# The context's exponentials in an attention loop: their low parts move from GpSimd to VectorE, behind the maxima

## The chip, the cores and the metric

The kernel runs on one core of a Trainium2 chip. A core has TensorE (matrix products, "PE" in the profile, with its weight loads "PEld"), VectorE ("DVE"), ScalarE ("ACT"), GpSimd ("POOL") and SyncE ("SP", which issues most DMAs here). Each has its own queue of instructions and works through it in order; between engines there are only semaphores. The metric is the device time of one execution in microseconds (us), the median over the runs shown.

## What is computed

One layer of an image generator: a modulated RMS norm, one input projection, two groups of heads, and one output projection added to the input. The part that matters here is the attention over 1024 tokens (a grid of 16 x 64) and 256 context tokens, with 8 heads of 64.

```python
s_lat = jnp.einsum('biqhd,birkhd->bhiqrk', q_rot, k_rows,
                   preferred_element_type=jnp.float32) * scale + bias
s_lat = jnp.where(col_valid[:, None, :], s_lat, -jnp.inf)
s_ctx = jnp.einsum('biqhd,blhd->bhiql', q_plain, kc,
                   preferred_element_type=jnp.float32) * scale
s = jnp.concatenate([s_lat.reshape(*s_lat.shape[:4], n_lat), s_ctx], axis=-1)
p = jax.nn.softmax(s, axis=-1).astype(v.dtype)
o = (jnp.einsum('bhiqrk,birkhd->biqhd', p_lat, v_rows)
     + jnp.einsum('bhiql,blhd->biqhd', p_ctx, vc))
```

Each query sees a window of neighbouring tokens (`s_lat`) and all context tokens (`s_ctx`) under one softmax. The other head group, a gated short convolution, and the gates of the attention are made of further columns of the input projection.

## The kernel before

**Precision.** Matrix products are made of three passes: each factor is split into a high part of a reduced type (`fp32r`) and a low part, the rest. So every matrix on chip costs a rounding copy (mostly on ScalarE) and a subtraction for the low part (mostly on VectorE). For the exponentials, ScalarE takes the exponential twice, once rounded into `ph` and once in full, and the low part is the full one minus `ph`.

**Stages.** Up to about 78 us the input is normed and transposed; up to about 258 us q, k and v are projected (`pacc`), normed and rotated; from there to about 529 us runs the attention, and the output projection (`pout`) from about 544 us to the end.

**The attention loop.** `quarter(n)` is called 36 times, four times for each head (a quarter is 256 queries) and four more at the end. It is a software pipeline of three heads' pieces: quarter `n` makes scores, quarter `e = n - 2` its exponentials, quarter `o = n - 3` the product with v. In each call, in this order as written:

- TensorE transposes the running maxima `mx` of quarter `e` into `pmx` (`pmx<-ci,mx`, two of 128 x 128); VectorE reduces them to `rm`.
- TensorE multiplies the context's exponentials of quarter `o` with v (`ctx_out`: `po<-phc,v` and `po<-plc,v`).
- VectorE does up to three waiting chores (`ul`, the low part of a weight; `cv`, the convolution's taps, and others).
- TensorE spreads `rm` over all partitions (`pmx<-ci,rm`), ScalarE copies it to `mg`; TensorE makes the scores `pss` of the window and `pc` of the context, ScalarE copies `pc` to `sc`.
- `ctx_exp`: VectorE subtracts the maximum from the context's scores (`sc<-sc,mg`), ScalarE takes the two exponentials (`phc`, then `sc` in place), and GpSimd subtracts them (`plc<-sc,phc`).
- The same for the window: VectorE `sb<-sb,mg`, ScalarE `phl` and `sb<-sb`.
- TensorE works on the fillers in between (`pu`: gates and convolution columns of the input projection, the weights loaded as `uraw`), and on `po<-phl,v`, `po<-pll,v`.
- VectorE adds the bias to the new scores (`sb<-pss,bt`) and takes the maxima of quarter `n`: `mx<-pc,sc`, with one input in PSUM, then two `mx<-mx,sb`, with both in SBUF.
- VectorE takes the window's low part (`pll<-sb,phl`).
- More fillers on TensorE, and the next call.

**The order.** In this stage the instructions of TensorE, ScalarE, VectorE and GpSimd stand in their queues just as the code calls them (`strict`, and `behind`, which ties each to the one ahead). The order of SP's DMAs is left to the scheduler. All of these calls go through a helper, so that the profile puts most of them down to its line 55; tiles are told apart by names. `phc` and `plc` have two buffers each, `sc` three.

Of the kernel before, what the change touches and what calls it, by code (L numbers as in the profile page):

```python
# [10 lines left out]
F32 = mybir.dt.float32  # L11
# [3 lines left out]
ALU = mybir.AluOpType  # L15
# [24 lines left out]
def body(tc, es, x, ctxt, w_ada, b_ada, w_in, q_g, k_g, rpbr, w_out, vecs, cst, out):  # L40
# [21 lines left out]
    pe, act, dve, pool = every = [ordered(e) for e in (nc.tensor, nc.scalar, nc.vector, nc.gpsimd)]  # L62
# [247 lines left out]
    def do_acts():  # L310
        for c in soon + (slow if not any(c[1] and c[1].__name__ == "product" for c in soon) else []):
            if c[0]:
                c[0]()
                c[0] = None

    def do_dves(most=99):
        for queue in chores:
            while queue and not queue[0][0] and (queue is soon or most > 0 and not soon):
                on_dve = queue.pop(0)[1]
                if on_dve:  # L320
                    on_dve()
                    most -= 1
# [632 lines left out]
    class head:  # L955
# [80 lines left out]
        def ctx_exp(self, g):  # L1036
            sc = self.cps[g]
            m = mg[:, g * 256:(g + 1) * 256].rearrange("p (o q) -> p o q", o=1)
            dve.tensor_tensor(sc, sc, m.broadcast_to([P, 2, 256]), ALU.subtract)
            ph = ap.tile([P, 2, 256], F32R, name="phc", tag="phc", bufs=2)  # L1040
            pl = ap.tile([P, 2, 256], F32R, name="plc", tag="plc", bufs=2)
            act.activation(ph, sc, AF.Exp)
            act.activation(sc, sc, AF.Exp)
            pool.tensor_tensor(pl, sc, ph[:].bitcast(F32), ALU.subtract)
            self.cps[g] = ph, pl

        def ctx_out(self, g):
            ph, pl = self.cps.pop(g)
            for i in range(2):
                self.pv(g // 2, slice((g % 2) * 256, (g % 2 + 1) * 256), NB + i, ph[:, i], pl[:, i], False)  # L1050
# [8 lines left out]
    def pair_of(n):  # L1059

        h, g = divmod(n, 4)
        two = [(h, 0), (h - 1, 7)] if g == 0 else [(h, 2 * g - 1), (h, 2 * g)]
        return [(i, heads[h_], j) for i, (h_, j) in enumerate(two) if 0 <= h_ < NH]

    def both(v, n, pair):

        w = 256 if n % 4 == 0 else 384
        return v[:, pair[0][0]:pair[-1][0] + 1, :w]

    def maxima_of(n, pair):  # L1070

        step, w = (768, 256) if n % 4 == 0 else (P, 384)
        lo = (2 * (n % 4) - 2) * P if n % 4 else pair[0][0] * step
        v = mg[:, lo:lo + w].rearrange("p (o c) -> p o c", o=1)
        if len(pair) == 1:
            return v
        part = list(v.ap)
        return bass.AP(v.tensor, v.offset, [part[0], [step, 2], [1, w]])

    def quarter(n):  # L1080

        live = lambda m: 0 <= m < 4 * NH
        ticks = TICKS[n]
        e, o = n - 2, n - 3
        if live(e):
            hd, g = heads[e // 4], e % 4
            pm = psm.tile([P, 512], F32, name="pmx", tag="C", bufs=2)  # L1090
            for i in range(2):
                pe.transpose(pm[:, i * P:(i + 1) * P], mx[:, (2 * g + i) * P:(2 * g + i + 1) * P], ident)
            rm = ap.tile([P, 2], F32, name="rm", tag="rm", bufs=8)
            dve.tensor_reduce(rm, pm[:, :256].rearrange("p (i k) -> p i k", i=2), AX.X, ALU.max)
        if live(o):
            heads[o // 4].ctx_out(o % 4)
        do_dves(3)
        if gating and next(gating[0], "end"):
            gating.pop(0)
        if live(e):  # L1100
            for i in range(2):
                pe.transpose(pm[:, 256 + i * P:256 + (i + 1) * P], rm[:, i:i + 1].broadcast_to([P, P]), ident)
            act.copy(mg[:, g * 256:(g + 1) * 256], pm[:, 256:512])
        now = pair_of(n)
        for i, hd_, j in now:
            hd_.scores(j, sbank[:, i])
        if n == 0:
            next(fill)
            ticks -= 1
        if live(n):  # L1110
            heads[n // 4].ctx_scores(n % 4)
        if live(e):
            hd.ctx_exp(g)
        if e in sbs or e in exps:
            pair, sb = pair_of(e), sbs.pop(e)
            w = both(sb, e, pair)
            dve.tensor_tensor(w, w, maxima_of(e, pair), ALU.subtract)
            exps[e] = [ap.tile([P, 2, 384], F32R, name=m, tag=m, bufs=2) for m in ("phl", "pll")]
            ph, pl = (both(v, e, pair) for v in exps[e])
            act.activation(ph, w, AF.Exp)  # L1120
            act.activation(w, w, AF.Exp)
        for _ in range(n > 0):
            next(fill, None)
        done = []
        if o >= 0:
            pho, plo = exps.pop(o)
            for i, hd_, j in pair_of(o):
                hd_.lat_out(j, pho[:, i], plo[:, i])
                if j in (4, 7):
                    done.append((hd_, j // 7))  # L1130
                    if j == 7 and hd_.s:
                        ready.append(hd_.p)
        if now:
            sb = sbs[n] = sb_new()
            g_ = n % 4
            if g_:
                bt = now[0][1].bt
                bias = bt[:, 1:2].broadcast_to([P, 2, 384]) if g_ == 2 else bt[:, 0:2] if g_ == 1 else bt[:, 1:3]
                dve.tensor_tensor(sb, sbank[:, :, :384], bias, ALU.add)
            else:  # L1140
                for i, hd_, j in now:
                    cols = slice(P, 384) if j == 0 else slice(0, 256)
                    dve.tensor_tensor(sb[:, i, :256], sbank[:, i, :256], hd_.bt[:, 1, cols], ALU.add)
            if live(n):
                heads[n // 4].ctx_max(n % 4)
            for i, hd_, j in now:
                hd_.lat_max(j, sb[:, i])
        if e in sbs or e in exps:
            dve.tensor_tensor(pl, w, ph.bitcast(F32), ALU.subtract)
        for _ in range(ticks - (n > 0)):  # L1150
            next(fill, None)
        for hd_, bank_ in done:
            hd_.finish(bank_)
        do_acts()
# [159 lines left out]
    with sbuf("att") as ap, psum("psb") as psb:  # L1314
# [6 lines left out]
        for n in range(4 * NH + 4):  # L1321
            h, g = divmod(n, 4)
            if 0 < h < NH and g == 0:
                heads[h].load_v()
            if h + 1 < NH and g:
                nx = heads[h + 1]
                for load in ((nx.masks, nx.load_q), (nx.load_k,), ())[g - 1]:
                    load()
            quarter(n)
            if ready:  # L1330
                p = ready.pop()
                if p < NPAIR - 1:
                    gating.append(gated(p))
                else:
                    recip(p, ap)
# [149 lines left out]
```

## Time and profile before

| | |
|---|---|
| median of 3 runs | 636.62 us (635.14 to 637.83) |
| the profiled execution | 636.35 us, of which its span 634.6 us |
| TensorE, matmuls | 626.0 us busy, 3503 instructions |
| TensorE, weight loads | 538.9 us |
| VectorE | 447.2 us, 832 instructions |
| ScalarE | 325.4 us, 701 instructions |
| GpSimd | 122.1 us, 134 instructions |
| the chain that ended last | PE 87%, DVE 6%, DMA 3% |

The page shows one execution. Busy time says how long an engine had an instruction in work; a matmul's end is modelled and neighbours overlap, so a busy TensorE is not one at its peak. A row of a group reads: line, engine, operation, output<-inputs, shape, count | busy us, mean ns of one | idle us of the engine just before them and what ended that. A row of the waits reads: who waited <- for whom: us in total, times, longest. A row of the timeline reads: start us, length us, engine, line, operation, tiles, shape, count [idle before <- what ended it].

### The profile page before, as it was taken

What the parts mean: (1) busy time and instruction counts of PE and PEld (TensorE: products, weight loads), DVE (VectorE), ACT (ScalarE), POOL (GpSimd) and SP (SyncE); (2) the same over time, 40 slices, a digit from 0 to 9 for tenths busy, and PEclk for the clock granted to TensorE, in tenths of its full rate; (3) what the DMA queues carried; (4) which work ended last, traced back from release to release, by engine and by line L of the source; (5) the groups of instructions that cost most, each with busy time, mean ns of one, the idle gap of its engine ahead of it and who ended that gap; (6) DMA issues with size and microseconds to landing.
All of it is one profiled execution on the core that took longest, in us unless ns stands there. A gap on an engine that the chain in (4) does not pass through costs nothing.

```text
span 634.6 us, 10089 instructions
## 1 busy us (share of the span) xinstructions
PE 626.0 (99%) x3503; PEld 538.9 (85%) x3504; DVE 447.2 (70%) x832; ACT 325.4 (51%) x701; POOL 122.1 (19%) x134
## 2 busy tenths in 40 slices
PE   8899999999999999999999999999999999999998
PEld 3577899999899999888888888888888888888887
DVE  1787858765766845568898889998998964577411
ACT  3677835423634545346576658566775845352000
POOL 1305014123123221101112111111111111003300
PEclk9999999999999999999999999999999999999999
DMA  8973638867684995875373636583742223965721
GB/s 312 372 252 127 185 108 258 255 196 228 233 273 131 299 327 174 295 254 161 134 256 124 237 102 211 174 295 93 254 148 78 60 92 123 309 211 176 253 101 50
DMA packets 103007, 125.61 MB, mean 198 GB/s; under 512 B 9665, under 2 KB 71577, under 8 KB 101676
## 3 DMA queue, kind: packets, MB, share of 16 engines
q1 hardware_dynamic: 96492, 113.38, 53.8%
q10 hardware_dynamic: 6208, 11.05, 5.5%
q0 software_dynamic: 256, 0.54, 0.3%
q8 instruction: 27, 0.44, 0.3%
q14 instruction: 24, 0.20, 0.1%
HBM read 88.09 MB, written 38.62 MB: 200 GB/s over the span
## 4 chain that ended last, share of the span: by engine, by line
PE 87%; DVE 6%; DMA 3%; ACT 1%; issue 1%; SPq 1%; DVEq 0%; ACTq 0%
PE pu L55 25%; PE pacc L55 21%; PE po L55 7%; PE acc L55 5%; PE pout L75 5%; PE pout L76 5%; PE pout L74 5%; PE cacc L55 4%; PE tr L55 3%; PE pss L55 3%; PE pmx L55 2%; DVE mx L55 2%; PE pc L55 2%; DMA slab<-in_w_ada 2%; DMA xx<-in_x 2%; DVE sb L55 2%
## 5 line engine op out<-in xcount | busy, mean ns | idle before, releaser
L55 PE MATMUL pu<-h,uh 128*128 128x512 f32 x544 | 169.0, 392 | 0.0
L55 PE MATMUL pacc<-wh,h 128*128 128x384 f32 x512 | 135.2, 338 | 0.0
L55 PEld LDWEIGHTS pu<-h,uh 128*128 128x128 f32 x544 | 98.1, 188 | 16.9
L55 PE MATMUL pu<-h,ul 128*128 128x512 f32 x272 | 106.3, 391 | 0.0
L55 PEld LDWEIGHTS pacc<-wh,h 128*128 128x128 f32 x512 | 92.8, 188 | 0.1
L55 PE MATMUL pacc<-wl,h 128*128 128x384 f32 x256 | 85.6, 334 | 0.0
L55 POOL TENSOR_TENSOR plc<-sc,phc 128x512 fp32r<-128x512 f32 x32 | 43.2, 1349 | 215.5 <-ACT sc L55 158.9
L55 POOL TENSOR_TENSOR ss<-ss,few 128x4 f32<-128x4 f32 (+1 forms) x40 | 41.5, 1039 | 126.3 <-DVE ss L55 126.1
L55 DVE TENSOR_TENSOR mx<-mx,sb 128x384 f32<-128x384 f32 (+1 forms) x64 | 59.5, 938 | 2.0
L55 PEld LDWEIGHTS pu<-h,ul 128*128 128x128 f32 x272 | 51.1, 188 | 11.3
L75 PE MATMUL pout<-wol,yh 128*128 128x512 f32 (+1 forms) x136 | 51.3, 377 | 0.0
L76 PE MATMUL pout<-woh,yl 128*128 128x512 f32 (+1 forms) x136 | 50.7, 377 | 0.0
L74 PE MATMUL pout<-woh,yh 128*128 128x512 f32 (+1 forms) x136 | 49.8, 377 | 0.0
L55 PEld LDWEIGHTS pacc<-wl,h 128*128 128x128 f32 x256 | 48.1, 188 | 0.1
L55 DVE TENSOR_REDUCE ss<-sq 128x4 f32<-128x260 f32 (+1 forms) x40 | 15.7, 394 | 42.1 <-ACT sq L55 42.0
L55 ACT ACTIVATE sq<-pacc 128x256 f32<-128x256 f32 x32 | 12.3, 385 | 54.5 <-PE pacc L55 54.1
L55 ACT COPY mg<-pmx 128x256 f32<-128x256 f32 x32 | 11.9, 373 | 51.9 <-PE pmx L55 47.4
L55 ACT COPY sc<-pc 128x512 f32<-128x512 f32 x32 | 18.9, 589 | 25.6 <-PE pc L55 25.6
L55 ACT ACTIVATE qn<-pacc,ss 128x64 f32<-128x64 f32 x128 | 30.1, 330 | 3.0 <-issue 2.5
L55 DVE TENSOR_TENSOR pll<-sb,phl 128x768 fp32r<-128x768 f32 (+2 forms) x33 | 28.4, 861 | 4.5 <-ACT sb L55 4.5
L55 PE MATMUL po<-phl,v 128*65 128x256 f32 (+2 forms) x160 | 31.2, 291 | 0.0
L75 PEld LDWEIGHTS pout<-wol,yh 128*128 128x128 f32 x136 | 25.6, 188 | 5.0 <-DVE wol L1364 0.3
(159 smaller groups left out, 1264.1 us busy)
## 6 DMA issues: line engine op xcount, KB each, us to landing
uraw<-in_w_in SPq DMA_DIRECT2D x34, 256.0 KB
q_d<-qs SPq DMA_DIRECT2D x32, 256.0 KB
k_s<-k_d SPq DMA_DIRECT2D x8, 1024.0 KB
q_s<-q_d SPq DMA_DIRECT2D x16, 512.0 KB
wr<-in_w_in SPq DMA_DIRECT2D x40, 192.0 KB
slab<-in_w_ada SPq DMA_DIRECT2D x6, 1024.0 KB
v_d<-vs SPq DMA_DIRECT2D x20, 260.0 KB
v<-v_d SPq DMA_DIRECT2D x16, 325.0 KB
```

The costliest lines, as they stand in the source:

```text
L55: i = emit(*a, **kw)
L74: i = pe.matmul(ps, ah, bh, start=first, stop=False)
L75: pe.matmul(ps, ah, bl, start=False, stop=False)
L76: pe.matmul(ps, al, bh, start=False, stop=last)
```

## The change

`ctx_exp` no longer gives GpSimd the subtraction `plc<-sc,phc`. It returns it as a function, and `quarter` calls this behind the maxima and ahead of the window's `pll`, on VectorE.

```diff
@@ ctx_exp
             act.activation(ph, sc, AF.Exp)
             act.activation(sc, sc, AF.Exp)
-            pool.tensor_tensor(pl, sc, ph[:].bitcast(F32), ALU.subtract)
             self.cps[g] = ph, pl
+            return lambda: dve.tensor_tensor(pl, sc, ph[:].bitcast(F32), ALU.subtract)
@@ quarter
         if live(e):
-            hd.ctx_exp(g)
+            ctx_rest = hd.ctx_exp(g)
...
                 heads[n // 4].ctx_max(n % 4)
             for i, hd_, j in now:
                 hd_.lat_max(j, sb[:, i])
+        if live(e):
+            ctx_rest()
         if e in sbs or e in exps:
             dve.tensor_tensor(pl, w, ph.bitcast(F32), ALU.subtract)
```

VectorE's queue, at the end of one quarter (the maxima, and the window's low part `pll`, then the next call's `rm`):

```order
 L55 TENSOR_TENSOR mx<-pc,sc 128x256
 L55 TENSOR_TENSOR mx<-mx,sb 128x384 x2
+L55 TENSOR_TENSOR plc<-sc,phc 128x512
 L55 TENSOR_TENSOR pll<-sb,phl 128x768
 L55 TENSOR_REDUCE rm<-pmx 128x2
```

One subtraction of 128 x 512 is added between the second maximum and `pll`; the 32 quarters with context exponentials have one each, and everything else on VectorE keeps its place.

TensorE's queue, in `ctx_out` of a quarter (`phc`, `plc`: high and low parts of the context's exponentials; in brackets the engines whose semaphore an instruction waits for):

```order
 L55 MATMUL po<-phc,v_3374 65x256 [waits Activation_49]
 L55 MATMUL po<-phc,v_3374 65x256
-L55 MATMUL po<-plc,v_3374 65x256 [waits Pool_49]
+L55 MATMUL po<-plc,v_3374 65x256 [waits DVE_49]
 L55 MATMUL po<-phc,v_3374 65x256 x2
 L55 MATMUL po<-plc,v_3374 65x256
```

The order on TensorE is the same; the product with the low part now waits for VectorE, not for GpSimd.

SP's queue, at the loads for a later head (`v`, `q_s`, `k_s`) around 440 us of the profile of before; `uraw` is a weight tile for the fillers:

```order
 L981 DMA v_3374<-v_d_100 128x650 x2
-L973 DMA q_s<-q_d_92 128x4x256
-L298 DMA uraw<-in_w_in 128x4x128
-L973 DMA q_s<-q_d_92 128x4x256
+L298 DMA uraw<-in_w_in 128x4x128
+L973 DMA q_s<-q_d_92 128x4x256 x2
 L966 DMA k_s<-k_d_96 128x1x2048
```

The load of `uraw` stood between the two halves of `q_s` and stands ahead of both now. ScalarE's queue keeps its order, and GpSimd's loses the 32 subtractions: between the last piece of the projections and the sums at the end there are only fills of `cu` (two columns at the edge of a convolution's input) left.

## The prediction

> **What bounds the kernel now.** I read the page's busy shares first, then the waits of TensorE in the stretch that the change touches (262 to 545 us, the attention), then the groups there, and last the timeline of single quarters of the loop.
>
> ```profile
> PE 626.0 (99%) x3503; PEld 538.9 (85%) x3504; DVE 447.2 (70%) x832; ACT 325.4 (51%) x701; POOL 122.1 (19%) x134
> 450.00:470.00 20.00, 19.99 (x122) 17.26 (x121) 19.64 (x31) 15.03 (x24) 2.60 (x2) 1.00 0.49 170
> PEld pmx L55 <- DVE rm L55: 3.1, 8, 0.8
> PEld pmx L55 <- ACT sb L55: 1.5, 3, 0.7
> PEld pmx L55 <- DVE mx L55: 1.1, 3, 0.6
> PE pmx L55 <- DVE rm L55: 1.0, 4, 0.5
> PE pmx L55 <- DVE mx L55: 0.7, 3, 0.3
> DVE rm L55 <- PE pmx L55: 12.9, 16, 2.1
> ```
>
> TensorE sets the time: 99% busy over the span. But VectorE runs close behind: in the row for 450 to 470 us (after the length come PE, PEld, DVE, ACT and POOL) it is busy 19.64 of 20 us. TensorE waits in the attention at one place only, the transposes `pmx`, in two halves: `pmx<-ci,mx` needs the running maxima, `pmx<-ci,rm` the reduced ones. Its weight loads wait 3.1 + 1.5 + 1.1 = 5.7 us there, its matmuls 1.0 + 0.7 = 1.7 us. Part of a load's wait lies under the matmul before it, so a faster VectorE can win between 1.7 and 5.7 us, 0.9% of the time at most. In 16 of 32 quarters `rm` itself waits for TensorE, 12.9 us in all; there VectorE has slack. The other 16 are those where VectorE runs without a pause up to `rm`.
>
> **The cost of the moved work.** What counts is not the GpSimd instruction's own time but what it does to VectorE beside it.
>
> ```profile
> L55 DVE TENSOR_TENSOR mx<-mx,sb 128x384 f32<-128x384 f32 x48 | 47.0, 979 | 1.6
> L55 DVE TENSOR_TENSOR mx<-mx,sb 128x256 f32<-128x256 f32 x16 | 12.5, 814 | 0.3
> L55 DVE TENSOR_TENSOR mx<-pc,sc 128x256 f32<-128x256 f32 x32 | 13.3, 416 | 1.0 <-ACT sc L55 0.9
> L55 POOL TENSOR_TENSOR plc<-sc,phc 128x512 fp32r<-128x512 f32 x32 | 43.2, 1349 | 215.5 <-ACT sc L55 158.9 <-PE po L55 31.3 <-issue 25.3
> L55 DVE TENSOR_TENSOR sc<-sc,mg 128x512 f32<-128x512 f32 x32 | 21.9, 684 | 9.8 <-ACT mg L55 9.8
> ```
>
> Rows of the timeline beside these groups (start, length, engine):
>
> ```profile
> 276.07 1.15 DVE L55 TENSOR_TENSOR mx<-mx,sb 128x384 f32<-128x384 f32 x2
> 304.28 1.29 POOL L55 TENSOR_TENSOR plc<-sc,phc 128x512 fp32r<-128x512 f32 x1 [6.22 <-ACT sc L55]
> 322.45 1.28 DVE L55 TENSOR_TENSOR ul<-uraw,uh 128x512 fp32r<-128x512 f32 x2
> 325.12 0.75 DVE L55 TENSOR_TENSOR sb<-pss,bt 128x256 f32<-128x256 f32 x2
> ```
>
> The maxima `mx<-mx,sb`, with both inputs in SBUF, take 979 ns for 384 elements and 814 for 256, while `mx<-pc,sc`, with one input in PSUM, takes 416 for 256. At 276.07, before the first GpSimd piece, two of 384 take 1.15 us together. At 304.51 (next part) two take 2.07 us, with the GpSimd piece running from 304.28 to 305.57. So the GpSimd piece stops the maxima while it runs. Priced by the two clean rows (0.575 us each of 384; 0.375 of 256, by the row of two at 325.12), the 64 maxima would take 27.6 + 6.0 = 33.6 instead of 47.0 + 12.5 = 59.5 us: **25.9 us** of VectorE come free.
>
> On the other side stand 32 subtractions of 512 elements on VectorE. The nearest rows are `sc<-sc,mg`, same shape and both inputs in SBUF, 684 ns, and a pair of `ul` that takes 1.28 us: one behind another adds 0.60. `plc` needs nothing of the maxima ahead of it, nor `pll` anything of `plc`, so I take 0.60, with 0.68 as the other end: 32 x 0.60 = **19.2 us** (21.9 at the other end). VectorE as a whole wins 6.7 us (4.0). GpSimd's 43.2 us cost nothing by themselves, nor is anything won there: what is left in its queue are the fills of `cu`, far ahead of their use.
>
> **What of it reaches the end.** Only quarters in which TensorE waited count, and there the two effects come one behind the other: the maxima end earlier, then `plc` stands ahead of `pll` and `rm`. An undelayed quarter has 0.92 us from the first `pmx<-ci,mx` to the first `pmx<-ci,rm` (first two rows).
>
> ```profile
> 299.77 0.38 PE L55 MATMUL pmx<-ci,mx 128*128 128x128 f32 x2
> 300.69 0.41 PE L55 MATMUL pmx<-ci,rm 128*128 128x128 f32 x2
> 304.51 2.07 DVE L55 TENSOR_TENSOR mx<-mx,sb 128x384 f32<-128x384 f32 x2
> 306.50 0.95 DVE L55 TENSOR_TENSOR pll<-sb,phl 128x768 fp32r<-128x768 f32 x1
> 307.37 0.42 DVE L55 TENSOR_REDUCE rm<-pmx 128x2 f32<-128x256 f32 x1
> 305.71 0.39 PE L55 MATMUL pu<-h,ul 128*128 128x512 f32 x1
> 306.14 0.30 PE L55 MATMUL pmx<-ci,mx 128*128 128x128 f32 x1
> ...
> 307.85 0.43 PE L55 MATMUL pmx<-ci,rm 128*128 128x128 f32 x2 [0.17 <-DVE rm L55]
> ```
>
> Quarter at 306: `rm` starts 0.87 us behind `pll`, TensorE's answer 0.48 behind `rm`, so `pll` plus 1.35. The maxima shrink from 2.07 to 1.15, `pll` moves by -0.92 + 0.60 = -0.32, and `pmx<-ci,rm` from 307.85 to 307.53. TensorE alone could be there at 305.71 + 0.39 + 0.92 = 307.02 at the latest: much of the wait stays, now on `rm` instead of on the maxima. **Gain 0.32.** The new wait of VectorE, `plc` on ScalarE's second exponential, holds up nothing: GpSimd, which waited for the same, started at 304.28, and `plc` starts at about 305.6. Behind it queue `pll` and `rm`. It ends about 306.3, ahead of its reader on TensorE, some 0.5 us behind the first `pmx`.
>
> The other delayed quarters go the same way, with one more limit: `pll` also waits for ScalarE's `sb<-sb`.
>
> ```profile
> 289.89 2.22 DVE L55 TENSOR_TENSOR mx<-mx,sb 128x384 f32<-128x384 f32 x2
> 292.20 0.38 PE L55 MATMUL pmx<-ci,mx 128*128 128x128 f32 x2
> 293.37 0.43 PE L55 MATMUL pmx<-ci,rm 128*128 128x128 f32 x2
> 326.24 1.67 DVE L55 TENSOR_TENSOR mx<-mx,sb 128x256 f32<-128x256 f32 x2
> 328.05 0.41 PE L55 MATMUL pmx<-ci,mx 128*128 128x128 f32 x2 [0.26 <-DVE mx L55]
> 329.16 0.43 PE L55 MATMUL pmx<-ci,rm 128*128 128x128 f32 x2
> 410.47 1.66 DVE L55 TENSOR_TENSOR mx<-mx,sb 128x384 f32<-128x384 f32 x2
> 471.76 1.67 DVE L55 TENSOR_TENSOR mx<-mx,sb 128x384 f32<-128x384 f32 x2
> 448.44 0.85 ACT L55 ACTIVATE sb<-sb 128x768 f32<-128x768 f32 x1
> 449.33 0.95 DVE L55 TENSOR_TENSOR pll<-sb,phl 128x768 fp32r<-128x768 f32 x1
> 504.11 0.84 ACT L55 ACTIVATE sb<-sb 128x768 f32<-128x768 f32 x1
> 505.10 0.94 DVE L55 TENSOR_TENSOR pll<-sb,phl 128x768 fp32r<-128x768 f32 x1
> ```
>
> - At 293: `pll` could move by -1.07 + 0.60 = -0.47; TensorE waited 293.37 - 292.20 - 0.92 = 0.25, all of it goes. **0.25.**
> - At 328: two of 256 shrink from 1.67 to 0.75; -0.92 + 0.60 = -0.32. TensorE waited 0.26 ahead of the first `pmx` and 329.16 - 328.05 - 0.92 = 0.19 behind it, more than that. **0.30**, a little taken off for ScalarE.
> - At 413 and 474: the GpSimd piece ran mostly beside instructions that it does not stop, the maxima took only 1.66 and 1.67, so just 0.51 and 0.52 are won and 0.60 paid. **Losses of 0.09 and 0.08**; two more quarters like them, without a wait so far, may add 0.05.
> - At 450 and 505: ScalarE ends `sb<-sb` at 449.29 and 504.95, and `pll` started at 449.33 and 505.10 already. ScalarE is late next, so only **0.04 and 0.15**.
>
> Sum: 0.25 + 0.32 + 0.30 + 0.04 + 0.15 - 0.09 - 0.08 - 0.05 = **0.84 us**. With 0.68 for each `plc` the two gains and four losses worsen by 0.08 each where the time of `plc` decides, and about 0.4 us is left. In the quarters with slack both effects lie under TensorE's own work.
>
> The moved step's DMAs: it issues none. In SP's queue one load of `uraw` now stands ahead of both halves of a `q_s`, not between them.
>
> ```profile
> 443.89 0.57 SPq L973 DMA_DIRECT2D q_s<-q_d  x1
> 445.06 0.38 SPq L298 DMA_DIRECT2D uraw<-in_w_in  x1
> ```
>
> That first half would leave 1.6 us later, behind `uraw`'s wait for its buffer. It is fetched for the next head, several quarters ahead (a quarter takes 6 to 8 us: their `pmx` start at 292.20, 299.77, 306.14), so I put it at nothing; if that cover were gone, it would cost the 1.6 us once.
>
> **The rivals.**
>
> *All waits go.* VectorE's lead of 6.7 us might carry over from quarter to quarter, so that it enters the late ones early. For it: 25.9 against 19.2 us. Against it: in half of the quarters `rm` waits for TensorE, and a lead ends there. It gives the middle between 1.7 and 5.7 us, 3.7 us: 632.9 us.
>
> *VectorE becomes the bound.* If the maxima are long for another reason than GpSimd, nothing is won, and the 16 quarters in which VectorE runs through to `rm` each pay 0.60 us: 9.6 us, 646.2 us. It decides as soon as a quarter wins less than the 0.60 that it pays; the quarters at 413 and 474 do so already. For it: VectorE at 19.64 of 20 us. Against it: the clean pair of 1.15 us, and that `mx<-pc,sc` beside the same GpSimd piece keeps its 416 ns.
>
> The Trainium skill speaks for this rival in its page Perfetto Trace Analysis, section Optimizing Scalar/DVE Operations: work may be taken off a saturated VectorE, even to GpSimd, and the change does the opposite. By that rule alone the 19.2 us go onto the busy engine and the 646.2 us come out. The same section warns that the two engines share a read port, so that moving work between them might not help; the rows of 2.07 against 1.15 us agree with the warning, not with the rule.
>
> *Nothing moves.* TensorE's 99% hide it all; the waits that are won come back one instruction later, behind ScalarE, as at 450 and 505 in every late quarter: 636.6 us.
>
> **How the numbers follow.** The profiled execution took 636.35 us, 634.6 of them span; the median of the runs is 636.62. The sum is made on the profiled one: 636.35 - 0.84 = 635.5, and against the median 635.8, which I predict. Chances: this forecast 0.48, all waits gone 0.22, VectorE as the bound 0.13, nothing moves 0.17. A measurement here can tell about 0.5%, 3.2 us. All waits gone is the only case beyond it on the fast side, 0.22; the bound is the one on the slow side, 0.13; the rest, 0.65, is within. The range takes in all waits gone below, and above the losing quarters, the `q_s` and the 1.2 us by which the runs of before exceed their median: 632.8 to 638.4, which leaves out the 0.13. The likeliest case alone has 634.6 to 637.
>
> **What would show it.** In the profile of the changed kernel: no `plc` on POOL; 32 of them on DVE at about 684 ns; `mx<-mx,sb` at about 560 to 580 ns for 384 elements, 410 for 256; DVE busy some 4 us less (durations overlap by 0.08 us, so busy time falls by less than the 6.7); the waits of `pmx` for `mx` nearly gone, those for `rm` still there. Maxima still near 979 ns, or PE waiting for `rm` in more than half of the quarters, would make the rival right. New waits of `po<-plc` for DVE would show the low part as late.

## The result, and the profile after

| | before | the change | ratio (95%) |
|---|---|---|---|
| median of 19 runs each | 636.29 us (635.01 to 638.22) | 634.77 us (633.94 to 636.73) | 0.9981 [0.9973, 0.9989] |
| the changed kernel in another series (17 and 11 runs) | 636.22 us | 635.40 us | 0.9988 [0.9978, 0.9998] |
| the profiled execution | 636.35 us, span 634.6 | 636.45 us, span 634.7 | |
| the attention stage in it | 235.52 us | 234.71 us | |

The change is faster by 0.1 to 0.2%, so by about 0.8 to 1.2 us; the forecast was 0.84, to a time of 635.8 us. That lies within the 0.5% that a measurement here was said to tell. The medians themselves lie 1.5 us apart in the one series and 0.8 in the other, so the times alone would not tell 0.84 us from twice as much; the profiles have to.

"The attention stage" is used throughout what follows: from the start of the first transpose of maxima (`pmx<-ci,mx`) to the start of the last of reduced maxima (`pmx<-ci,rm`). Both stand on TensorE, which sets the time, and the one stretch holds 31 of the 32 subtractions that the change moves; the last comes behind it, at 516 us of the changed kernel, and from the stage's end to the output projection both kernels take 29.4 us. The rows are the first and last of each profile (start in us, length, engine); before, then the change:

```profile
278.88 0.38 PE L55 MATMUL pmx<-ci,mx 128*128 128x128 f32 x2
...
514.40 0.42 PE L55 MATMUL pmx<-ci,rm 128*128 128x128 f32 x2
```

```profile
278.31 0.38 PE L55 MATMUL pmx<-ci,mx 128*128 128x128 f32 x2
...
513.02 0.41 PE L55 MATMUL pmx<-ci,rm 128*128 128x128 f32 x2
```

514.40 - 278.88 = 235.52 and 513.02 - 278.31 = 234.71: the stage became 0.81 us shorter. A difference of two spans would have shown nothing here (634.6 and 634.7), since the rest of the program differs between executions by more than the change brings. That is taken up under the second run of the kernel before.

The busy line of the changed kernel, its groups on VectorE in the attention (262 to 545 us; behind the bar come busy us, mean ns of one, idle us ahead of them), and its waits:

```profile
PE 625.3 (99%) x3503; PEld 539.0 (85%) x3504; DVE 440.7 (69%) x864; ACT 325.3 (51%) x701; POOL 79.0 (12%) x102
```

```profile
L55 DVE TENSOR_TENSOR mx<-mx,sb 128x384 f32<-128x384 f32 x48 | 26.8, 559 | 1.7
L55 DVE TENSOR_TENSOR plc<-sc,phc 128x512 fp32r<-128x512 f32 x32 | 21.9, 685 | 0.5 <-ACT sc L55 0.5
L55 DVE TENSOR_TENSOR mx<-pc,sc 128x256 f32<-128x256 f32 x32 | 13.3, 415 | 1.0 <-ACT sc L55 0.9
L55 DVE TENSOR_TENSOR mx<-mx,sb 128x256 f32<-128x256 f32 x16 | 6.2, 423 | 0.3
```

```profile
DVE rm L55 <- PE pmx L55: 19.5, 21, 2.1
PEld pmx L55 <- DVE rm L55: 4.1, 7, 0.8
PE pmx L55 <- DVE rm L55: 2.1, 5, 0.5
```

VectorE has 32 instructions more (832 to 864) and is busy 6.5 us less (447.2 to 440.7). The maxima of 384 elements went from 979 to 559 ns, those of 256 from 814 to 423; `mx<-pc,sc`, with one input in PSUM, kept its 415. What VectorE won shows up as idle time: `rm` now waits for TensorE 19.5 us in 21 quarters, where it was 12.9 us in 16. TensorE no longer waits for `mx` in the transposes, and a little more of its matmuls' time goes to `rm` (2.1 us, from 1.0). Add up these waits and the matmuls seem to have lost 0.4 us (1.7 to 2.1) while the stage won 0.81: a wait that moves from one instruction to the next changes its share that lies under the work ahead. What a quarter wins is read from the distance between two rows, not from the list of waits.

### The profile page after: what moved, and what is told of

Same layout as the page of the kernel before. It is cut to its first block, busy times and chain, and to the rows that moved or that the text cites. A ratio compares the mean times of both kernels' runs of the same rounds, so it can differ in the third digit from the quotient of the medians.

```text
span 634.7 us, 10005 instructions
## 1 busy us (share of the span) xinstructions
PE 625.3 (99%) x3503; PEld 539.0 (85%) x3504; DVE 440.7 (69%) x864; ACT 325.3 (51%) x701; POOL 79.0 (12%) x102
## 4 chain that ended last, share of the span: by engine, by line
PE 77%; DMA 6%; issue 6%; DVE 5%; ACT 3%; SPq 1%; POOL 1%; ACTq 0%; DVEq 0%; POOLq 0%
PE pu L55 24%; PE pacc L55 21%; PE po L55 6%; PE acc L55 4%; PE cacc L55 4%; PE pss L55 3%; PE tr L55 3%; PE pmx L55 2%; PE pc L55 2%; PE pout L75 2%; PE pout L76 2%; PE pout L74 2%; DMA slab<-in_w_ada 2%; DMA xx<-in_x 2%; DMA xr<-in_x 1%
## 5 line engine op out<-in xcount | busy, mean ns | idle before, releaser
L55 DVE TENSOR_TENSOR mx<-mx,sb 128x384 f32<-128x384 f32 (+1 forms) x64 | 33.0, 525 | 2.0
L74 PEld LDWEIGHTS pout<-woh,yh 128*128 128x128 f32 x136 | 25.6, 188 | 5.8 <-ACT yh L1388 0.9
```

The source lines that it names most:

```text
L55: i = emit(*a, **kw)
L74: i = pe.matmul(ps, ah, bh, start=first, stop=False)
```

## The experiments

All figures for a stage are of one profiled execution of each kernel. Each ratio is taken to runs of the kernel before in the same series, whose medians lay between 635.86 and 636.33 us. The expectations count the stage to the second product of its last pair, 0.14 us more. In them, `pll` is the window's low part, `plc` the context's. A quarter is named by the time of its `pmx` in the kernel before, to within about 1 us (449 and 450 are one).

| kernel | time, us | ratio to before (95%) | stage, us |
|---|---|---|---|
| before | 636.29 | | 235.52 |
| the change | 634.77 | 0.9981 [0.9973, 0.9989] | 234.71 |
| again: the change | 635.40 | 0.9988 [0.9978, 0.9998] | 234.71 |
| before_again: before | 637.77, one run | | 235.53 |
| none: no `plc` anywhere | 633.40 | 0.9961 [0.9949, 0.9972] | 233.33 |
| both: `plc` on both engines | 644.57 | 1.0136 [1.0123, 1.0150] | 243.88 |
| early: `plc` on VectorE at its old place | 675.18 | 1.0607 [1.0579, 1.0635] | 275.38 |
| swap: `plc` behind `pll` | 638.41 | 1.0033 [1.0018, 1.0047] | 238.14 |
| late_a: the change, `pll` behind `rm` | 635.59 | 0.9996 [0.9983, 1.0008] | 235.14 |
| late_b: before, `pll` behind `rm` | 640.01 | 1.0062 [1.0046, 1.0078] | 239.03 |
| pick: `pll` behind `rm` in two quarters | 634.80 | 0.9974 [0.9963, 0.9985] | 234.59 |
| pick2: and `plc` on GpSimd in two | 634.42 | 0.9973 [0.9962, 0.9985] | 234.39 |
| pick3: one quarter, and two | 634.59 | 0.9977 [0.9966, 0.9988] | 233.77 |

### Is the stage's 0.81 us the change, and the rest the execution?

*again* is the changed kernel, unaltered.

> The changed kernel once more. Theory (attention wins about 0.8 us by itself, the rest of the difference is spread of the executions): from the first to the last pmx transposes 234.9 us within 0.3, as in the first profile of the change (235.7 before), and 634 to 636 us. In that first profile the output projection stood still twice, 0.8 + 1.0 us between matmuls at 568 and 592 us. If these pauses belong to the execution, they are gone or elsewhere here. Rival (the change gives its gain back in the output projection): both pauses stand at the same places again.

*before_again* is the kernel before, unaltered, in one execution.

> The kernel before once more, for its output projection. Its first profile had 87.4 us from the first to the last product of the output projection, with no pause; four of the kernels since had 88.1 to 89.8 us, with pauses at about 26 and 50 us behind the first product. Theory (the pauses belong to the execution, not to the change): pauses of that kind here too, 88 to 90 us, and again 235.7 us within 0.3 from the first to the last pmx. Rival (the change moves its gain into the output projection): 87.4 us and no pause again.

The stage repeats: 234.71 us both times for the change, 235.52 and 235.53 for the kernel before. The single quarters repeat too, none differing by more than 0.03 us between the two profiles of the change. What does not repeat is the output projection at the end. The rows of its first product (shortest, median and longest in ns, then the first and last start) in the kernel before and in its second execution:

```profile
L74 PE MATMUL pout<-woh,yh x136: 277/389/395, 543.8 to 631.0; 128*128 128x512 f32 x120, 128*128 128x256 f32 x16
```

```profile
L74 PE MATMUL pout<-woh,yh x136: 277/390/502, 543.0 to 632.4; 128*128 128x512 f32 x120, 128*128 128x256 f32 x16
```

and in the changed kernel:

```profile
L74 PE MATMUL pout<-woh,yh x136: 278/389/497, 542.4 to 631.1; 128*128 128x512 f32 x120, 128*128 128x256 f32 x16
```

From first to last start that is 87.2 us, 89.4 and 88.7. The change's profiled execution came to the projection 1.4 us early (0.57 us already at the start of the stage, 0.81 in it) and lost 1.5 us there, in pauses such as the first row below; the same kind of pause stands in the second execution of the kernel before, the second row.

```profile
592.44 0.50 PE L75 MATMUL pout<-wol,yh 128*128 128x512 f32 x1 [0.55 <-DVE wol L1366]
```

```profile
593.74 0.50 PE L75 MATMUL pout<-wol,yh 128*128 128x512 f32 x1 [0.55 <-DVE wol L1364]
```

So the equal spans of the two profiles shown first are no sign that the win was given back: those pauses come and go with the execution, with either kernel. What decides them stays open.

### The two sides of the trade, one at a time

*none* takes the subtraction away from both engines. The output leaves out the low part of the context's exponentials, with the high part in its place in the third product, so TensorE's work stays as it was.

```diff
-            pl = ap.tile([P, 2, 256], F32R, name="plc", tag="plc", bufs=2)
...
-            self.cps[g] = ph, pl
-            return lambda: dve.tensor_tensor(pl, sc, ph[:].bitcast(F32), ALU.subtract)
+            self.cps[g] = ph, ph
+            return lambda: None
```

> Leaves out the low part plc on every engine; the third product of the context takes the high part instead. Theory (GpSimd's piece stopped the maxima, VectorE's piece costs 0.60 us a quarter): maxima of 384 near 560 ns as in the changed kernel; the attention wins about 2.0 us against before, so 233.6 us from the first to the last pmx, some 634.3 us in all; what is left of the waits for rm stands behind ScalarE. Rival (all waits of TensorE go with VectorE's load): 3.5 us or more won, 632.9 us. Rival (VectorE's load does not matter): no difference to the changed kernel.

*both* keeps the subtraction on VectorE and gives it to GpSimd as well.

```diff
             act.activation(sc, sc, AF.Exp)
+            pool.tensor_tensor(pl, sc, ph[:].bitcast(F32), ALU.subtract)
             self.cps[g] = ph, pl
```

> The low part is taken twice, on GpSimd as before and again on VectorE behind the maxima. Theory (GpSimd's reading stops the maxima): maxima of 384 back at about 980 ns in the order of the changed kernel, VectorE 26 us busier than there, and every quarter in which VectorE ran through to rm pays 0.60 us: 8 to 11 us slower than before, 645 to 647 us. Rival (the maxima were long for another reason, gone with the new order): maxima near 560 ns and 635 us.

The group of the large maxima and TensorE's wait for `rm`, in *none* and then in *both*:

```profile
L55 DVE TENSOR_TENSOR mx<-mx,sb 128x384 f32<-128x384 f32 x48 | 26.8, 559 | 1.7
...
PEld pmx L55 <- DVE rm L55: 2.6, 5, 0.8
```

```profile
L55 DVE TENSOR_TENSOR mx<-mx,sb 128x384 f32<-128x384 f32 x48 | 46.3, 965 | 1.6
...
PEld pmx L55 <- DVE rm L55: 11.9, 21, 0.8
```

The maxima are long with GpSimd's subtraction beside them (965 ns in *both*) and short without it (559 in *none*, 559 in the change), whether or not VectorE has a `plc` of its own. That settles what stops them. With it the change splits into two parts: taking GpSimd's piece away shortens the stage by 235.52 - 233.33 = 2.19 us, putting `plc` on VectorE lengthens it again by 234.71 - 233.33 = 1.38. Of the 1.38, four quarters hold 1.26: 0.54 us at 474, 0.43 at 306, 0.21 at 413, 0.08 at 328. In *both*, where `plc` is paid and nothing is won for it, the stage takes 8.36 us more than before, and TensorE's loads wait for `rm` in 21 quarters. So the prediction's rival of VectorE as the bound had about the right price (9.6 us), though not its terms: 19 quarters lose 0.13 to 0.59 us each, where it had 16 at 0.60. What kept it away is the relief alone. In *both* the two engines also write the same tile, and VectorE's `plc` waited for GpSimd's once within the stage, 1.30 us in the quarter at 450; that quarter lost 0.35 us, no more than others.

### The place in the queue

*early* has `plc` on VectorE where GpSimd's call used to stand, right behind the exponentials.

```diff
             self.cps[g] = ph, pl
-            return lambda: dve.tensor_tensor(pl, sc, ph[:].bitcast(F32), ALU.subtract)
+            dve.tensor_tensor(pl, sc, ph[:].bitcast(F32), ALU.subtract)
...
-        if live(e):
-            ctx_rest()
```

> VectorE takes the low part at the place of the GpSimd instruction, ahead of the window's subtraction, so in front of ScalarE's two exponentials' end. Theory (the place behind the maxima is what makes it cheap): VectorE stands about 1.3 us in each quarter until the exponentials are there, the window's exponentials and maxima all come later: 10 to 25 us slower than before, 646 to 662 us. Rival (only the load counts): the time of the changed kernel, 634 to 636 us.

The time rose by 39 us (6.07%), where 25 were the most that was expected. The waits, and the place in one quarter:

```profile
DVE plc L55 <- ACT sc L55: 55.3, 32, 2.6
ACT phl L55 <- DVE sb L55: 52.8, 33, 3.1
PEld pmx L55 <- ACT sb L55: 24.1, 21, 2.8
```

```profile
287.59 0.69 DVE L55 TENSOR_TENSOR sc<-sc,mg 128x512 f32<-128x512 f32 x1 [0.33 <-ACT mg L55]
...
290.18 0.69 DVE L55 TENSOR_TENSOR plc<-sc,phc 128x512 fp32r<-128x512 f32 x1 [1.90 <-ACT sc L55]
290.79 0.95 DVE L55 TENSOR_TENSOR sb<-sb,mg 128x768 f32<-128x768 f32 x1
```

Between `sc<-sc,mg` and `plc` ScalarE has to take two exponentials, and VectorE stands for 1.90 us. Over the 32 quarters it is 1.36 to 2.58 us each, more than the 1.3 that were expected. The second row of the waits goes with it: behind `plc` in VectorE's queue stands `sb<-sb,mg`, which the window's exponentials on ScalarE need. So ScalarE stands as well, in every quarter, and each engine waits in turn for the other. Not all of these waits reach the end: the stage grew by 39.9 us. How that divides between the two engines' waits stays open.

*swap* has `plc` one place later than the change, behind `pll`.

```diff
-        if live(e):
-            ctx_rest()
         if e in sbs or e in exps:
             dve.tensor_tensor(pl, w, ph.bitcast(F32), ALU.subtract)
+        if live(e):
+            ctx_rest()
```

> The changed kernel with plc behind pll instead of ahead of it; both stay ahead of rm. Theory (only the sum ahead of rm counts, except where pll waits for ScalarE): the same stage within 0.5 us, 634.9 to 635.4 from the first to the last pmx taken as 234.9 to 235.4 us, the quarters at 449 and 504 worse by up to 0.6 us each since plc then also stands behind ScalarE's last exponential. Rival (plc is needed at once by TensorE and must stand first): po waits for plc in most quarters, 3 us or more slower.

The rival was right in its size and its cause, though TensorE waits for `plc` in seven quarters only, not in most: 0.33% slower than before, the stage 3.43 us longer than in the change. The quarter at 505 in *swap*:

```profile
506.30 0.48 PE L55 MATMUL po<-phc,v 128*65 128x256 f32 x2
506.36 0.96 DVE L55 TENSOR_TENSOR pll<-sb,phl 128x768 fp32r<-128x768 f32 x1 [0.83 <-ACT sb L55]
507.23 0.69 DVE L55 TENSOR_TENSOR plc<-sc,phc 128x512 fp32r<-128x512 f32 x1
507.97 0.34 PE L55 MATMUL po<-plc,v 128*65 128x256 f32 x1 [1.20 <-DVE plc L55]
```

`pll` waits for ScalarE, `plc` stands behind it, and TensorE's third product of the context, which comes right behind the first two, waits 1.20 us. In seven quarters this makes 4.6 us of waiting matmuls. In the change `plc` runs, in the same quarter, while ScalarE still works on `sb<-sb`:

```profile
502.78 0.69 DVE L55 TENSOR_TENSOR plc<-sc,phc 128x512 fp32r<-128x512 f32 x1
502.83 0.85 ACT L55 ACTIVATE sb<-sb 128x768 f32<-128x768 f32 x1
503.70 0.96 DVE L55 TENSOR_TENSOR pll<-sb,phl 128x768 fp32r<-128x768 f32 x1 [0.24 <-ACT sb L55]
```

So its place ahead of `pll` costs nothing there. Over the stage that place is worth 3.4 us. Not every quarter has the wait for ScalarE: at 306 `pll` starts in *swap* with none, and TensorE waits 0.81 us for `plc` all the same, since `plc` comes later by the time of `pll`.

### Taking `pll` out of the way of `rm`

What was left in the change were waits for `rm`, which stands behind `plc` and `pll`. *late_a* holds `pll` back until the next quarter's `rm` is out; *late_b* does the same to the kernel before.

```diff
             dve.tensor_reduce(rm, pm[:, :256].rearrange("p (i k) -> p i k", i=2), AX.X, ALU.max)
+        while lows:
+            lows.pop()()
...
         if e in sbs or e in exps:
-            dve.tensor_tensor(pl, w, ph.bitcast(F32), ALU.subtract)
+            lows.append(lambda: dve.tensor_tensor(pl, w, ph.bitcast(F32), ALU.subtract))
```

> The changed kernel with the window's low part pll taken behind rm, not ahead of it. Theory (what is left of TensorE's waits is rm standing behind pll, and pll behind ScalarE): the waits of pmx for rm, 4.1 us of weight loads in the changed kernel, nearly go; 232.5 us from the first to the last pmx against 234.9, some 632.5 to 633 us. Rival (pll, now behind rm's own wait for TensorE, comes late for the next subtractions): the waits come back at mx, and the time is that of the changed kernel or above, 635 to 637 us.

> The kernel before (low part on GpSimd) with pll behind rm. Theory (in the late quarters TensorE waits for rm behind pll, and only in four of them also for the maxima): the waits for rm go, those for the maxima, about 1.5 us, stay: about 233.8 us from the first to the last pmx, 634.5 us, so between the changed kernel and the one with both edits. Rival: as for the one above, 636 us or more.

The theory fell. *late_a* is not to be told from before (0.9996 [0.9983, 1.0008]), *late_b* is 0.62% slower. TensorE's wait for `rm` did go, as it was meant to, and VectorE now stands ahead of `rm`; then the fillers' work behind it is late. The rival had the time right, but of the new waits of TensorE's matmuls in *late_a* only 0.4 us are for `mx`, and 0.7 for `cv`. The waits, and the place at 484 us, of *late_a*:

```profile
DVE rm L55 <- PE pmx L55: 31.5, 26, 2.5
...
PEld pmx L55 <- DVE rm L55: 0.8, 1, 0.8
```

```profile
481.51 0.42 DVE L55 TENSOR_REDUCE rm<-pmx 128x2 f32<-128x256 f32 x1 [1.83 <-PE pmx L55]
481.85 0.95 DVE L55 TENSOR_TENSOR pll<-sb,phl 128x768 fp32r<-128x768 f32 x1
482.71 0.69 DVE L55 TENSOR_TENSOR ul<-uraw,uh 128x512 fp32r<-128x512 f32 x1
483.32 1.28 DVE L55 TENSOR_TENSOR cv<-pu,cv 128x512 f32<-128x512 f32 x2
484.06 0.73 PE L55 MATMUL pu<-h,uh 128*128 128x512 f32 x2 [0.47 <-DVE cv L55]
```

VectorE waits 1.83 us for TensorE with `pll` ready to run behind the waiting instruction. Then `pll`, `ul` and `cv` come in a row, and a filler on TensorE waits for `cv`. The quarter at 490 alone lost 0.75 us against the change. So `pll` ahead of `rm` is a good use of the time in which `rm` must wait anyway, in most of the quarters where its place matters: against the change *late_a* won at 450, 474 and 505 and lost in six others. Why *late_b* lost more, 3.5 us of the stage, stays open.

### Only where it pays

*pick* holds `pll` back in two quarters only (449 and 505), those with the largest wait left behind ScalarE's `sb<-sb`.

```diff
-            dve.tensor_tensor(pl, w, ph.bitcast(F32), ALU.subtract)
+            low = lambda: dve.tensor_tensor(pl, w, ph.bitcast(F32), ALU.subtract)
+            lows.append(low) if e in (22, 29) else low()
```

> The changed kernel with pll behind rm in two quarters only, those at 449 and 505 us where pll stands waiting for ScalarE. Theory (there rm waits behind ScalarE, and nowhere else does pll behind rm pay): the quarters at 449 and 505 win 0.35 and 0.62 us against the changed kernel, as they did with pll behind rm everywhere, the others keep their times: 233.9 us from the first to the last pmx against 234.85, 633.5 to 634.5 us. Rival (the late pll pushes the work behind it into the quarters that follow): 234.5 us or more.

At 505 it won 0.62 us against the change and at 449 0.34, but the quarter behind 449 lost 0.86, so the rival was right. Rows of *pick* for it:

```profile
448.79 0.95 DVE L55 TENSOR_TENSOR pll<-sb,phl 128x768 fp32r<-128x768 f32 x1
449.65 0.68 DVE L55 TENSOR_TENSOR cu<-pu,ub 128x512 f32<-128x512 f32 x1
...
456.91 0.42 DVE L55 TENSOR_REDUCE rm<-pmx 128x2 f32<-128x256 f32 x1
457.38 0.43 PE L55 MATMUL pmx<-ci,rm 128*128 128x128 f32 x2 [0.52 <-DVE rm L55]
```

`pll` takes 0.86 us from its start to the next one, and VectorE then waits for nobody up to the next `rm`: there is no slack in this quarter, and the 0.86 come out at its end.

*pick2* also leaves `plc` on GpSimd in the two quarters where the change lost.

```diff
             self.cps[g] = ph, pl
+            if 4 * self.h + g in (17, 25):
+                pool.tensor_tensor(pl, sc, ph[:].bitcast(F32), ALU.subtract)
+                return lambda: None
```

> The same, and in two quarters the low part of the context stays on GpSimd: those ahead of rm at 412 and 473 us, where the change lost. Theory (the losses of 0.09 and 0.15 us there are VectorE's piece against a shorter stop by GpSimd): both quarters back at the time before, 0.24 us won against the one above, 233.7 us for the stage; too small to be seen in the times. Rival (the overlap with GpSimd has moved, now that VectorE is earlier): no gain in these two quarters or a loss.

The two quarters came back, 0.13 and 0.16 us against *pick*: there GpSimd's piece really was the cheaper one. *pick3* keeps that, and of *pick* only the quarter at 505.

```diff
-            lows.append(low) if e in (22, 29) else low()
+            lows.append(low) if e == 29 else low()
```

> The changed kernel with pll behind rm only in the quarter at 505 us, and the low part of the context on GpSimd only ahead of the quarters at 412 and 473 us. Theory (each quarter can be priced by itself from the runs so far): 0.6 us won at 505, 0.09 and 0.15 us at 412 and 473, nothing lost elsewhere: 234.0 us from the first to the last pmx, some 2.2 us under the median of before, 634 us. Rival (an edit at one quarter shifts the ones behind it, as at 457 us in the two kernels above): 234.5 us or more.

Its stage is 233.77 us, 1.75 less than before and 0.94 less than the change, close to what was forecast. Its time (ratio 0.9977 [0.9966, 0.9988]) is below the time before, and not to be told from the change's own (0.9981 [0.9973, 0.9989]). That it beats the change rests on the stage of one profile.

## Why the prediction was right, point by point

**What bounds the kernel.** TensorE does: it is 98 or 99% busy in every profile but that of *early* (95%). VectorE's time counts in single quarters only. *none* shows how small a part that is: VectorE loses the stalls, 26.5 us by its groups, pays nothing, and the stage wins 2.19.

**What stops the maxima.** Right, and shown by *both* and *none*. The Trainium skill states it in its page SBUF — State Buffer, section Who interferes with whom: an instruction of VectorE with two inputs in SBUF contends with one of GpSimd that reads SBUF. The rows agree: 979 ns with the piece and 559 without it, while `mx<-pc,sc` keeps 415.

**The cost of the moved work.** 25.9 us were to come free; the two groups fell from 59.5 to 33.0 us, 26.5. For `plc` 0.60 us were taken and 0.68 kept as the other end; start to start it is 0.61 in the quarter at 306, shown next. VectorE's win was put at 6.7 us, and its busy time fell by 6.5. The remark that it would fall by some 4 us only, since durations overlap, was wrong: the page's busy time does not count an overlap twice, the sums of the groups do (59.5 - 33.0 - 21.9 = 4.6).

**The quarters.** The quarter at 306 in the changed kernel:

```profile
303.69 1.16 DVE L55 TENSOR_TENSOR mx<-mx,sb 128x384 f32<-128x384 f32 x2
304.76 0.69 DVE L55 TENSOR_TENSOR plc<-sc,phc 128x512 fp32r<-128x512 f32 x1
305.37 0.95 DVE L55 TENSOR_TENSOR pll<-sb,phl 128x768 fp32r<-128x768 f32 x1
306.23 0.42 DVE L55 TENSOR_REDUCE rm<-pmx 128x2 f32<-128x256 f32 x1
305.12 0.38 PE L55 MATMUL pmx<-ci,mx 128*128 128x128 f32 x2
306.71 0.43 PE L55 MATMUL pmx<-ci,rm 128*128 128x128 f32 x2 [0.51 <-DVE rm L55]
```

The pair of maxima takes 1.16 us for 2.07, `plc` adds 0.61, and the wait is now on `rm`, as the prediction had it. What each quarter won is the change of the distance between its `pmx<-ci,rm` and that of the quarter ahead:

| quarter | forecast, us | measured, us |
|---|---|---|
| 293 | -0.25 | -0.26 |
| 306 | -0.32 | -0.32 |
| 328 | -0.30 | -0.30 |
| 450 | -0.04 | -0.03 |
| 505 | -0.15 | -0.19 |
| 413 | +0.09 | +0.09 |
| 474 | +0.08 | +0.15 |
| two more (458 and 490) | +0.05 | +0.02 |
| sum | -0.84 | -0.84 (the stage: -0.81) |

The other quarters moved by 0.03 us or less each, and make up the difference to the stage. The single terms are what bears the prediction out; that the sums agree to the last digit is luck, since the misses cancel. The largest, 0.07 us, is at 474. The prediction's picture of 413 and 474, a GpSimd piece mostly beside instructions that it does not stop, was a little off too: at 413 the piece ran from 409.84 to 411.13 and the maxima began at 410.47, so about half of it fell on them. The 0.51 and 0.52 us were read from the maxima themselves and stand. At 474 VectorE has no pause from one `rm` to the next, so whatever else takes longer counts too: of the 0.15, 0.08 come from the trade between maxima and `plc`, as worked out, and 0.07 from a pair of `cv` ahead of them in the fillers, which took 1.60 us in place of 1.53.

**The queues.** The swapped loads of `q_s` and `uraw` were priced at nothing. No quarter shows a loss that the working above leaves over, so no 1.6 us were paid. Nor does the list of waits have a product that waits for `plc`, which was to be the sign of a late low part; at 306 `plc` ended at 305.45, ahead of its reader at 305.57.

**The rivals.** *All waits go* asked for 3.7 us. It did not happen because the lead ends at `rm`: the win of VectorE, 6.5 us, reappears as 6.6 us more of waiting there (12.9 to 19.5). *VectorE becomes the bound* is what *both* is, 8.36 us in the stage where 9.6 were worked out. The point from which it decides held: the quarters at 413 and 474, which won less than 0.60, lost. The Trainium skill's rule of taking work off a saturated VectorE (page Perfetto Trace Analysis, section Optimizing Scalar/DVE Operations) would, taken alone, have had the change lose; the trace does not bear it out here, as the pieces on GpSimd cost VectorE 26.5 us and doing them 21.9 at most. *Nothing moves* is refuted by the stage, repeated to 0.01 us, and by both intervals, which stay below 1, the second of them barely (0.9998).

## What to carry to other kernels

An offloaded instruction is priced by what it takes from the engine beside it: compare the neighbour's rows with and without it, here, in the quarter at 306, 0.92 us of stall against 0.60 us of doing the work. Then count only the quarters in which the engine that sets the time waits, and look for the next thing that is late there; 26.5 us of stalls were worth 2.2 us of the stage. In an in-order queue, an instruction whose input another engine has still to make belongs behind work that is ready, and ahead of the next instruction that must wait anyway: ahead of `sb<-sb,mg`, the bias and the maxima, `plc` cost 39 us here; one place too late, behind `pll`, 3.4.

## What was not expected of the hardware

The stop works in both directions. In the kernel before, where a maximum had started first, GpSimd's piece became longer too (row of 311), 1.58 us, where the one that started ahead of the maxima took 1.29:

```profile
311.32 2.13 DVE L55 TENSOR_TENSOR mx<-mx,sb 128x384 f32<-128x384 f32 x2
311.46 1.58 POOL L55 TENSOR_TENSOR plc<-sc,phc 128x512 fp32r<-128x512 f32 x1 [5.88 <-ACT sc L55]
```

What one GpSimd piece costs VectorE hangs on what it meets: 0.92 to 1.07 us at 293, 306 and 328, where most of it fell on the maxima, 0.51 and 0.52 at 413 and 474, where its first half ran beside instructions with an input in PSUM. With the piece back on GpSimd in these two quarters, *pick2* shows it again, 1.62 us for the pair of maxima where the change has 1.15 (quarter at 413):

```profile
407.62 1.30 POOL L55 TENSOR_TENSOR plc<-sc,phc 128x512 fp32r<-128x512 f32 x1 [19.21 <-PE po L55]
407.87 0.41 DVE L55 TENSOR_TENSOR mx<-pc,sc 128x256 f32<-128x256 f32 x1
408.31 1.62 DVE L55 TENSOR_TENSOR mx<-mx,sb 128x384 f32<-128x384 f32 x2
```

That is why two quarters were better off with GpSimd, and why the best stage here (*pick3*) leaves it the piece in these two.
